# Hybrid mLSTM and attention layer: the four t1 token sums of the block products given lags of 2.7 instead of 1.5

## The chip, the cores and the metric

The kernel runs on one core of a Trainium2 chip. The metric is the device time of one execution in microseconds (us). The kernel before has three timed runs and one profiled run.

## What is computed

One step of a decoder layer, for a prompt of 1024 tokens and for 8 sample sequences of 4 tokens (32 rows), with a model width of 1024. The input is normalised and modulated (adaLN) to h. One wide product `h @ w_in` gives the inputs of two branches, an mLSTM with 4 heads and matrix memory, and sliding window attention with 8 heads; gates merge the two, and an output product closes the layer:

```python
h, gate = adaln_in(x, c, w_ada, b_ada, g_norm)
(mq, mk, mv, mi, mf, mo, mz, aq, ak, av, az, gm, ga) = split_in(h @ w_in)
y_m, C, n, m = mlstm_branch(mq, mk, mv, mi, mf, mo, mz, C0, n0, m0, b_i, b_f, g_mn)
...
y_a = o.astype(x.dtype) * jax.nn.silu(az)
u = jax.nn.sigmoid(gm) * (y_m @ w_mo) + jax.nn.sigmoid(ga) * (y_a @ w_ao)
x = x + gate * (u @ w_o)
```

Within a head the mLSTM goes through the prompt in chunks of 128 tokens. For each chunk there is a masked score product S of queries and keys, an output n from S and from the memory C, and an update U of C. The sample rows take their memory from `state_C` and `state_n` and give it back.

## The kernel before, in words

Products with large weights run in float32r at full rate with each operand split into a high and a low part (names with `h` and `l`), as three products: high by high, low by high, high by low. ACT makes a high part by a cast, and DVE the low part by a subtraction. A product of 512 columns is one PE instruction of 128 x 128 weights.

The kernel has four stages: the normalisation and the first products; direct jobs (queries and head inputs, `head_jobs`); the block products (`block_products`, from line 1493), which run from about 285 to 820 us on the profile's clock and include everything told here; and the output product.

**Block products.** The columns of `w_in` that are left are taken in pairs of 128 column blocks. The 2 x 2 form by Strassen and Winograd over halves of the contraction (kh) and of the tokens (th) needs 7 products instead of 8. They are numbered 1 to 7, and `flat` lists them in PE's order; a product is called (pair, number), as (0,5). Each has 12 matmuls: three for each of four k. Their right operands are blocks of h (b11, b21, b22) and four sums of token blocks, t1 to t4. Results stand in PSUM tiles bx, bw, by and bz; `samples` (line 1356) makes the sample rows of a pair as 16 small matmuls into `smp`, ACT copies that to `smps`, and a further small matmul makes `smpo` from it. `evac` empties a finished product: for head inputs DVE adds two parts into `mkv`, for gates ACT makes a tanh into `gt`; `gts` is the same for the sample rows. The left operands, weights (`wr_...`), come by DMA, are summed by DVE (`first_sums`, line 1370) and split into `wh_...` and `wl_...` with a number for the product.

**The token sums.** `sum_blocks` (line 1302) forms t3, t2 and t4 first, then t1. t1 is formed in place over block (0,1) of h, so it waits until the direct jobs, which read that block, are done (`products_done`, set at line 1815). Then for each of four k: ACT casts the high part, DVE subtracts it for the low part (`block_split`, line 1294), and for the first two k the loads of a later pair of `hb` tiles are issued. Behind each of the four stands a lag.

**The side work.** Between the k of a product, `side.tick` (class `Side`, lines 112 to 170) lets other work into PE's order: the heads of the mLSTM, at most two at once, the attention, the sample heads, the output weights (`out_weights`, line 1743) and `sum_blocks` itself. Each is a Python generator; what it yields is a lag and the PSUM banks of its next step. The clock of this scheduler, `now`, is a model: each matmul that is written adds its own modelled time (512 columns: 512 / 2400 us). A step is taken when its lag has passed, its banks are free by the model and 1.5 us have passed since the last one with banks. A loop holds the main products where they need a result:

```python
def until(self, done):
    while not done():
        self.now += 0.1
        self.tick()
...
if n == 0 and i in (6, 5):
    side.until(lambda: {6: "t2", 5: "t1"}[i] in formed)
```

The second part is in `hook` (line 1786), which every product calls first. So ahead of (0,5) the clock goes on in steps of 0.1 until t1 is formed, and side steps that come due meanwhile are written into PE's order there.

PE runs in the order in which the program is written (`in_order`). DVE and ACT, in this stage, are ordered by the tile scheduler from the program's order and its own estimates. All loads and stores go through SP's queue in order, and each also waits for the landing of the eighth before it. A store is held back by 8 us of the model's clock, or until its data is read.

**A head's chunk** has, on PE, tk and tv (transposes of keys and values, copied to `hk` and `hv` by ACT), S, U and n, and later ty (transposes of the output). DVE updates C from U, prepares the mask tile `et` and the weighted query `qw`, which come by DMA (`et<-nmd`, `qw<-wid`, and `hq`, `hk`, `hv`), and scales the output with a reciprocal square root in small steps (f3r_w, f3r_y). ACT takes the exponential of et. tk, tv, ty, smp, smpo and sU share one pool of two PSUM banks (pool b), so each waits until the one before the last has been copied out. A sample head has, on PE, sn (reads the memory Cs) and three sU (its update), and DVE adds them, `Cs<-Cs,sU`.

`out_weights` loads pairs of tiles `wor` and scales them by the gate on DVE (`wor<-wor,gb`).

Of the kernel before, what the change touches and what calls it, by code (L numbers as in the profile page):

```python
# [172 lines left out]
def body(tc, a):  # L173
    nc = tc.nc
    with ExitStack() as ctx:
# [810 lines left out]
        def head_jobs(h):  # L986
            q, k, v = mD[h]

            def keep(dst, smp, scale, eng):
                def ev(p, acc, c0, n):  # L990
                    t = ht([128, 384], f"mk{h}")[:, :n]
                    if eng == "v":
                        V.tensor_copy(t, acc[:, :n])
                    else:
                        S.activation(t, acc[:, :n], AF.Copy, scale=scale)
                    m = n if p < 2 else 256
                    store(dst[:, c0:c0 + m], t[:, :m])
                    if p == 2:
                        G.tensor_copy(smp[:, h], t[:, 256:288])
                return ev  # L1000

            for n, dst, smp, scale in (("mq", q, qs, float(128 ** -0.5)), ("mk", k, ks, 1.0), ("mv", v, vs, 1.0)):
                if (n, h) not in order:
                    return
                i = order.index((n, h)) - order.index(None)
                if i == -4:
                    side.add("x", sum_blocks())
                if i == -1:
                    side.finish("g")
                    sc_bank[:] = po, "o+"  # L1010
                    next(work)
                job((n, h), keep(dst, smp, scale, "s"), (lambda: next(work)) if i == -1 else None)
                head_part(h, 2)
# [273 lines left out]
        def block_load(names, k):  # L1287
            ts = []
            for kh, th in names:
                ts.append(ht([128, 512], f"hb{kh}{th}_{k}"))  # L1290
                dma(ts[-1], hD[:, 4 * kh + k, HALF[th]])
            return ts

        def block_split(n, k, t):
            hi, lo = blocks[n][k]
            S.copy(hi, t)
            V.tensor_tensor(lo, t, hi.bitcast(F32), op=ALU.subtract)

        def block_tiles(n, k):
            blocks[n].append(tuple(ht([128, 512], f"{n}{x}{k}", F32R) for x in "hl"))  # L1300

        def sum_blocks():
            names = "t3", "t2", "t4"
            for n in names:
                blocks[n] = []
            load = lambda k: block_load(((0, 0), (0, 1), (1, 0), (1, 1)), k)
            nxt = load(0)
            yield 7.0, ""
            for k in range(4):
                b11, b12, b21, b22 = nxt  # L1310
                for n in names:
                    block_tiles(n, k)
                V.tensor_tensor(b22, b22, b12, op=ALU.subtract)
                yield 2.5, ""
                V.tensor_tensor(b11, b11, b22, op=ALU.add)
                V.tensor_tensor(b21, b21, b11, op=ALU.subtract)
                yield 5.0, ""
                if k < 3:
                    nxt = load(k + 1)
                for n, t in zip(names, (b22, b11, b21)):  # L1320
                    block_split(n, k, t)
                    yield 2.5, ""
            formed.append("t2")
            load = lambda k: block_load(((0, 0), (0, 1)), k)
            ts = [load(0), load(1)]
            yield 3.0, ""
            for b11, b12 in ts:
                V.tensor_tensor(b12, b12, b11, op=ALU.subtract)
            while not products_done:
                yield 0.5, ""  # L1330
            for k in range(4):
                b11, b12 = ts[k]
                if k > 1:
                    V.tensor_tensor(b12, b12, b11, op=ALU.subtract)
                block_split("t1", k, b12)
                if k < 2:
                    ts.append(load(k + 2))
                yield 1.5, ""
            formed.append("t1")

        OPERANDS = {1: "b11", 2: "b21", 3: "b22", 4: "t4", 5: "t1", 6: "t2", 7: "t3"}
# [1 line left out]
        class Pair:  # L1343
# [6 lines left out]
            def load(self):  # L1350
                for c, n in enumerate(self.names):
                    for kh in range(2):
                        t = self.raw[c, kh] = raw_tile(f"wr_{n[0]}{n[1]}_{kh}")
                        dma(t, a["w1"][JOBS[n]][:, 4 * kh:4 * kh + 4])
# [819 lines left out]
```

## Time and profile before

| what | us |
|---|---|
| timed runs | 847.02, 848.38, 848.36 |
| median of the timed runs | 848.36 |
| the profiled run's own time | 845.97 |
| span of the profiled run | 844.1 |
| DVE busy in the span | 574.6 (68%) |
| ACT busy in the span | 399.9 (47%) |

The span goes from the first to the last instruction. The granted clock of TensorE has a mean of 0.997. Rows of a timeline give the start, the busy time, the engine and line, the operation with output and inputs, the number of instructions in the group, and in brackets how long the engine was idle ahead of it and what ended that. All operations of DVE and ACT have line 219 and the matmuls lines 258 and 263, those of the helpers that record them, so a group is known by its tiles. float32r shows as f32 in PE's rows.

### The profile page before, as it was taken

How to read it: one execution, taken by the hardware profiler on the slowest of the kernel's cores; microseconds unless marked ns; L12 is line 12 of the kernel's file. 1: busy time of each engine (PE TensorE's matmuls, PEld its weight loads, DVE VectorE, ACT ScalarE, POOL GpSimd, SP SyncE). 2: the span in 40 equal slices, each digit the busy share in tenths (PEclk: the TensorE clock that was granted, in tenths of full speed). 3: DMA queues.
4: the chain of work that ended last, by engine and by line, in shares of the span. 5: the costliest groups of instructions: out<-in, count | busy, mean ns of one | idle time of the engine just before them, and what ended most of it. 6: DMA issues, size and time to landing. Idle time of an engine off the chain costs nothing.

```text
span 844.1 us, 15344 instructions
## 1 busy us (share of the span) xinstructions
PE 826.2 (98%) x5231; PEld 692.9 (82%) x5231; DVE 574.6 (68%) x1554; ACT 399.9 (47%) x989; POOL 43.9 (5%) x77
## 2 busy tenths in 40 slices
PE   6999999999999999999999999999999999999996
PEld 3779999879988878888878777777778999997776
DVE  4887884556666586655776776788876767844676
ACT  4663346555764454554444534444444333234343
POOL 0120000000000000000000000000001202240000
PEclk9999999999999999999999999999999999999998
DMA  9996548348755653456656574555444698343532
GB/s 334 381 353 196 145 149 280 111 125 259 213 158 171 191 172 119 153 162 175 199 184 224 172 241 127 177 165 138 126 145 148 209 333 292 105 129 121 200 107 106
DMA packets 120417, 158.16 MB, mean 187 GB/s; under 512 B 27520, under 2 KB 71168, under 8 KB 120308
## 3 DMA queue, kind: packets, MB, share of 16 engines
q1 hardware_dynamic: 120196, 156.93, 58.0%
q8 instruction: 41, 0.67, 0.3%
q14 instruction: 36, 0.29, 0.1%
q10 hardware_dynamic: 144, 0.26, 0.1%
HBM read 113.41 MB, written 44.75 MB: 187 GB/s over the span
## 4 chain that ended last, share of the span: by engine, by line
PE 86%; DVE 6%; DMA 4%; issue 2%; ACT 1%; SPq 1%; DVEq 0%; ACTq 0%
PE bx L258 9%; PE by L258 8%; PE bw L258 8%; PE g_aq L258 6%; PE g_w_mo L258 6%; PE g_w_ao L258 5%; PE g_mk L258 4%; PE g_mq L258 4%; PE bz L258 4%; PE g_mv L258 3%; PE foW L258 3%; PE foX L258 3%; PE foY L258 2%; PE sc L258 2%; PE oT L258 2%; PE foZ L258 2%
## 5 line engine op out<-in xcount | busy, mean ns | idle before, releaser
L258 PE MATMUL g_w_ao<-ya,wh_w_ao 128*128 128x384 f32 (+1 forms) x192 | 45.6, 322 | 0.1
L258 PE MATMUL g_w_mo<-ym_l,wh_w_mo 128*128 128x384 f32 (+1 forms) x192 | 45.7, 323 | 0.0
L219 ACT ACTIVATE p<-p,nmx 128x256 f32<-128x256 f32 (+1 forms) x64 | 31.0, 486 | 27.0 <-DVE nmx L219 22.8
L258 PEld LDWEIGHTS g_w_ao<-ya,wh_w_ao 128*128 128x128 f32 x192 | 33.5, 188 | 0.6 <-DVE ya L219 0.4
L258 PEld LDWEIGHTS g_w_mo<-ym_l,wh_w_mo 128*128 128x128 f32 x192 | 33.5, 188 | 0.0
L258 PE MATMUL g_aq<-h_h,wh_aq 128*128 128x384 f32 (+1 forms) x96 | 32.4, 337 | 0.0
L258 PE MATMUL g_aq<-h_l,wh_aq 128*128 128x384 f32 (+1 forms) x96 | 31.0, 323 | 0.0
L258 PE MATMUL g_w_mo<-ym_l,wl_w_mo 128*128 128x384 f32 (+1 forms) x96 | 31.0, 323 | 0.0
L258 PE MATMUL g_aq<-h_h,wl_aq 128*128 128x384 f32 (+1 forms) x96 | 31.0, 323 | 0.0
L258 PE MATMUL g_w_ao<-ya,wl_w_ao 128*128 128x384 f32 (+1 forms) x96 | 30.8, 321 | 0.0
L219 DVE CUSTOM_DVE_ANT_0 p<-sc,cst,sink 128x256 f32<-128x256 f32 (+1 forms) x64 | 26.1, 464 | 3.9 <-PE sc L258 3.9
L258 PE MATMUL g_mk<-h_h,wh_mk 128*128 128x384 f32 (+1 forms) x72 | 24.8, 344 | 0.0
L258 PE MATMUL g_mq<-h_h,wh_mq 128*128 128x384 f32 (+1 forms) x72 | 24.4, 339 | 0.0
L219 ACT ACTIVATE gt<-gt 128x512 f32<-128x512 f32 (+1 forms) x17 | 10.4, 613 | 29.0 <-DVE gt L219 27.8
L258 PE MATMUL g_mk<-h_l,wh_mk 128*128 128x384 f32 (+1 forms) x72 | 23.3, 323 | 0.0
L258 PE MATMUL g_mq<-h_l,wh_mq 128*128 128x384 f32 (+1 forms) x72 | 23.3, 323 | 0.0
L258 PE MATMUL g_mk<-h_h,wl_mk 128*128 128x384 f32 (+1 forms) x72 | 23.2, 323 | 0.0
L258 PE MATMUL g_mq<-h_h,wl_mq 128*128 128x384 f32 (+1 forms) x72 | 23.2, 323 | 0.0
L219 DVE SCALAR_TENSOR_TENSOR u_h<-tgw_ao,g_w_ao 128x384 f32<-128x384 f32 (+1 forms) x24 | 12.3, 519 | 11.4 <-PE g_w_ao L258 11.0
L258 PEld LDWEIGHTS g_aq<-h_h,wh_aq 128*128 128x128 f32 x96 | 18.0, 188 | 1.4 <-issue 1.2
L219 DVE SCALAR_TENSOR_TENSOR tgw_mo<-tgw_mo,g_w_mo 128x384 f32<-128x384 f32 (+1 forms) x24 | 12.4, 518 | 9.6 <-PE g_w_mo L258 9.4
L219 ACT ACTIVATE sq<-rows_l 128x512 f32<-128x512 f32 (+2 forms) x18 | 10.6, 587 | 17.8 <-issue 12.0
(1718 smaller groups left out, 2695.8 us busy)
## 6 DMA issues: line engine op xcount, KB each, us to landing
hb<-hD SPq DMA_DIRECT2D x24, 256.0 KB
x<-xT SPq DMA_DIRECT2D x16, 256.0 KB
early_h<-w_ada SPq DMA_DIRECT2D x8, 512.0 KB
adar_ga<-w_ada SPq DMA_DIRECT2D x16, 256.0 KB
wr_ga<-w SPq DMA_DIRECT2D x16, 256.0 KB
wr_gm<-w SPq DMA_DIRECT2D x16, 256.0 KB
taD<-gt SPq DMA_DIRECT2D x16, 256.0 KB
tmD<-gt SPq DMA_DIRECT2D x16, 256.0 KB
```

What stands on the lines that cost most here:

```text
L219: ins = f(*args, **kw)
L258: in_order(nc.tensor.matmul(out, lhsT, rhs, start=start, stop=stop, skip_group_check=more))
```

## The change

One line of `sum_blocks`: the lag behind each of the four steps that form t1 is 2.7 instead of 1.5.

```diff
                 block_split("t1", k, b12)
                 if k < 2:
                     ts.append(load(k + 2))
-                yield 1.5, ""
+                yield 2.7, ""
             formed.append("t1")
```

The same instructions are written with the same shapes. Their order changes from (0,5) to the end of the sample heads; ahead of that and in the output product it is the same. Three places follow.

The first is DVE at the start of the block products, around the emptying of by (`mkv<-p,by`), which the product (0,4) needs. `et` and `qw` with `cst` and `hq` are the preparation of the next chunk. Before:

```order
L219 TENSOR_TENSOR f3r_w<-f3r_y 128x3
L219 TENSOR_TENSOR f3r_w<-f3r_w,f3v 128x3
L219 SCALAR_TENSOR_TENSOR f3r_y<-f3r_w,f3r_y 128x3
L219 TENSOR_SCALAR et<-et,f3den,f3r_y 128x128 x3
L219 TENSOR_TENSOR ws_4131<-wr_gm_0_4030,wr_gm_1_4032 128x512
L219 TENSOR_TENSOR wl_phead_in_6__3971<-wr_mk_0_3679,wh_phead_in_6__3970 128x512
L219 TENSOR_TENSOR mkv<-p_3915,by 128x512
L219 SCALAR_TENSOR_TENSOR C<-C,dec,U_1_3920 128x129 x3
```

And now:

```order
L219 SCALAR_TENSOR_TENSOR f3r_y<-f3r_w,f3r_y 128x3
L219 TENSOR_TENSOR et<-et,cst 128x256
L219 TENSOR_TENSOR f3r_w<-f3r_y 128x3
L219 SCALAR_TENSOR_TENSOR C<-C,dec,U_1_3898 128x129
L219 TENSOR_TENSOR f3r_w<-f3r_w,f3v 128x3
L219 TENSOR_TENSOR qw<-qw,hq_2_3911 128x256
L219 SCALAR_TENSOR_TENSOR f3r_y<-f3r_w,f3r_y 128x3
L219 SCALAR_TENSOR_TENSOR C<-C,dec,U_1_3898 128x129
L219 TENSOR_SCALAR et<-et,f3den,f3r_y 128x128 x3
L219 TENSOR_TENSOR ws_4152<-wr_gm_0_4033,wr_gm_1_4035 128x512
L219 TENSOR_TENSOR wl_phead_in_6__3988<-wr_mk_0_3679,wh_phead_in_6__3987 128x512
L219 TENSOR_TENSOR mkv<-p_3943,by 128x512
```

The updates of C, which stood behind mkv, stand ahead of it (the first of the three just ahead of these rows), and one et and one qw as well, which stood some rows further on.

The second is ACT in the last chunk of head 3, in the products of a gate pair; gts is the copy of smpo and frees its bank. Before:

```order
L219 CAST wh_pgate_3__5307<-wr_ga_1_4902 128x512
L219 COPY by<-bw 128x512
L219 ACTIVATE gts<-smpo 128x64
L219 ACTIVATE et<-et,an 128x128 x2
L219 ACTIVATE yt<-ty_0_5268,vec 128x384
L219 CAST wh_pgate_4__5331<-wr_gm_1_4906 128x512
```

And now:

```order
L219 ACTIVATE et<-et,an 128x128 x2
L219 CAST wh_pgate_3__5307<-wr_ga_1_4908 128x512
L219 COPY by<-bw 128x512
L219 ACTIVATE gts<-smpo 128x64
L219 ACTIVATE yt<-ty_0_5258,vec 128x384
L219 CAST wh_pgate_4__5332<-wr_gm_1_4912 128x512
```

The two exponentials of et, which stood behind gts, stand ahead of wh_3, by and gts.

The third is PE at the first sample head, in the products of pair 6's gate. Before:

```order
L258 MATMUL smp<-wr_gm_0_5961,c_102 32x128
L258 MATMUL smp<-wr_gm_1_5963,c_102 32x128
L258 MATMUL sU_0_6056<-vm_5859,skn 128x388
L258 MATMUL sU_1_6059<-vm_5864,skn 128x388
L258 MATMUL by<-t3h_2714,wh_pgate_7__5965 128x512
L258 MATMUL by<-t3l_2715,wh_pgate_7__5965 128x512
L258 MATMUL by<-t3h_2714,wl_pgate_7__5966 128x512
```

And now:

```order
L258 MATMUL bx<-h_h_576,wl_pgate_2__5935 128x512
L258 MATMUL sU_0_6028<-vm_5848,skn 128x388
L258 MATMUL sU_1_6031<-vm_5853,skn 128x388
L258 MATMUL bx<-h_h_576,wh_pgate_2__5934 128x512
L258 MATMUL bx<-h_l_577,wh_pgate_2__5934 128x512
L258 MATMUL bx<-h_h_576,wl_pgate_2__5935 128x512
L258 MATMUL smp<-wr_ga_0_5981,c_102 32x128
```

The first two sU stood behind the 16 matmuls of smp (the first two rows are the last of these); now they stand three matmuls ahead of smp (the last row is its first matmul). On DVE the addition `Cs<-Cs,sU` follows the fourth `wor<-wor,gb` directly; before, a `wl` and a weight sum stood between them. On SP, the loads of a head's next chunk and the weight loads have changed places: in head 3 the loads hq, hk, hv, et and qw now follow directly on `wr_ga` of pair 5's first half, ahead of a store of tmD and of its second half, which stood ahead of them before; and the last pair of hb loads for t1 now stands behind the second half of pair 0's gate weight `wr_ga`, where it stood ahead of it.

## The prediction

> **What bounds the kernel now.** I read the page first, then the waits of PE, then the timelines of the engines around each place that the change moves. The page has PE busy for 826.2 of 844.1 us at a granted clock that stays at nine tenths or more in all slices but the last:
>
> ```profile
> PE 826.2 (98%) x5231; PEld 692.9 (82%) x5231; DVE 574.6 (68%) x1554; ACT 399.9 (47%) x989; POOL 43.9 (5%) x77
> ...
> PEclk9999999999999999999999999999999999999998
> ```
>
> So PE sets the end: a matmul that waits costs its whole wait, and a wait on another engine costs only where PE's row stands behind it. From 280 to 830 us, which holds everything that the change moves, PE waits three times (the columns are total, times, longest):
>
> ```profile
> PE smp L258 <- ACT hv L219: 1.9, 1, 1.9
> PE bx L258 <- ACT gt L219: 0.5, 1, 0.5
> PE sU L258 <- DVE Cs L219: 0.2, 1, 0.2
> ```
>
> That is 2.6 us. No more than this, and the price of switching between kinds of matmul, can be gained. What can be lost is not bounded so: the three rows say that all other waits just fit now.
>
> **What the change does.** It adds no instruction's work and removes none. The four lags only move the side clock: while the loop in `hook` waits for t1 at product (0,5), the clock is pushed ahead by up to 4.8 us more (4 x 1.2), so every side block behind it becomes due earlier. On PE, the blocks of the heads stand three to ten matmuls ahead of where they stood, until the sample heads end. The operands of these blocks come from DVE, ACT and SP, whose order moves too. Six places have a price.
>
> *1. The first product with t4, by(0,4).* PE ends bw(0,3) and then waits a little for DVE's `mkv`, which empties `by`:
>
> ```profile
> 307.37 0.69 DVE L219 TENSOR_TENSOR mkv<-p,by 128x512 f32<-128x512 f32 x1
> 307.97 1.12 DVE L219 SCALAR_TENSOR_TENSOR C<-C,dec,U 128x129 f32<-128x129 f32 x3
> ```
>
> ```profile
> 307.59 0.39 PE L258 MATMUL bw<-h_h,wl_phead_in__3879 128*128 128x512 f32 x1
> 308.11 0.50 PE L258 MATMUL by<-t4h,wh_phead_in__3898 128*128 128x512 f32 x1
> ```
>
> bw's last matmul holds PE for 0.23 us (the spacing shown under 4), to 307.82; by starts at 308.11, so 0.29 is lost. Now three updates of C (1.03 from 307.97 to the next operation), one `et` and one `qw` (0.43 each, by the row of that shape under 5) stand ahead of `mkv` on DVE: 1.9 in all. Part of it falls into the chain of small f3r steps, each of which waits for the one before it, so I take half, 0.9: mkv ends at 308.95. PE meanwhile has ty_0, 0.33, ahead of by instead of inside it, and comes to by at 308.15. The loss is 0.85 instead of 0.29: **+0.6**. Bounds: all hidden, -0.3; nothing hidden, +1.6.
>
> *2. tv of head 2, chunk 0*, now directly behind smp and tk, needs the bank that ACT frees by copying smps; tk's three matmuls cover 0.33 of that copy and its start. **+0.2**, between 0 and 0.4.
>
> *3. Gate pair 0.* n, tk, tv and S of head 2, chunk 1 now stand three matmuls ahead of smp instead of behind it, and smp takes the bank that `hv<-tv` frees. This is the mechanism of the 1.9 us wait above. How long hv takes from tk shows one chunk later in the kernel before (ACT, then PE):
>
> ```profile
> 321.44 0.35 ACT L219 COPY hv<-tv 128x256 f32<-128x256 f32 x1
> ...
> 325.56 0.48 ACT L219 COPY hv<-tv 128x384 f32<-128x384 f32 x1 [1.92 <-PE tv L263]
> ```
>
> ```profile
> 319.82 0.38 PE L263 MATMUL tk<-cst,hk 128*128 128x128 f32 x2
> ```
>
> From tk to the end of hv are 321.79 - 319.82 = 1.97, and 0.13 more for the copy of three parts. PE's own tk, tv, S and three matmuls come to about 2.0. **+0.2**, from 0 up to 0.7 if ACT is late.
>
> *4. Fewer switches.* The first 512 column matmul behind a block of small ones has its next 0.32 behind it, all others 0.23:
>
> ```profile
> 418.14 0.48 PE L258 MATMUL bw<-t2h,wh_pgate__5147 128*128 128x512 f32 x1
> 418.46 0.39 PE L258 MATMUL bw<-t2l,wh_pgate__5147 128*128 128x512 f32 x1
> 418.69 0.40 PE L258 MATMUL bw<-t2h,wl_pgate__5148 128*128 128x512 f32 x1
> ```
>
> The changed order has five such blocks fewer (they now follow another block directly). 5 x 0.09: **-0.45**. That is certain, since the order is fixed.
>
> *5. Head 3, last chunk, around 416 to 427 us.* SP's queue, DVE, ACT and PE before:
>
> ```profile
> 415.22 0.33 SPq L246 DMA_DIRECT2D wr_ga<-w  x1
> ...
> 418.43 0.42 SPq L246 DMA_DIRECT2D et<-nmd  x1
> ```
>
> ```profile
> 424.21 0.43 DVE L219 TENSOR_TENSOR et<-et,cst 128x256 f32<-128x256 f32 x1 [5.95 <-DMA et<-nmd]
> ```
>
> ```profile
> 418.93 0.62 ACT L219 CAST wh_pgate__5307<-wr_ga 128x512 fp32r<-128x512 f32 x1
> 419.46 0.58 ACT L219 COPY by<-bw 128x512 f32<-128x512 f32 x1
> 419.97 0.21 ACT L219 ACTIVATE gts<-smpo 128x64 f32<-128x64 f32 x1
> 424.67 0.70 ACT L219 ACTIVATE et<-et,an 128x128 f32<-128x128 f32 x2 [4.49 <-DVE et L219]
> ```
>
> ```profile
> 422.34 0.30 PE L258 MATMUL smp<-wr_ga,c 128*32 128x128 f32 x2
> ```
>
> The load of et, issued at 418.43, reaches DVE at 424.21: 5.78 us. ACT took wh_3, by and gts while it was under way. In the changed order ACT has the two `et` activations ahead of these three, so ACT stands still until et has landed; gts frees the bank of smp, so PE stands still with it. The load itself is issued earlier: on SP it now follows that wr_ga at 415.22 by four issues of some 0.45, so at about 417.0. From landing to gts pass 0.46 (DVE), 0.60 (two et), 0.53 (wh), 0.51 (by), 0.21 (gts) and the release: 2.35. With 5.78 from issue to landing, smp would start at 417.0 + 5.8 + 2.35 = 425.1 instead of 422.34, 2.8 later. The shortest time of such a load is in these two rows (SP, DVE), 3.83:
>
> ```profile
> 310.61 0.41 SPq L246 DMA_DIRECT2D et<-nmd  x1
> ```
>
> ```profile
> 314.44 0.56 DVE L219 TENSOR_TENSOR et<-et,cst 128x384 f32<-128x384 f32 x1 [1.75 <-DMA et<-nmd]
> ```
>
> With that, 423.2: 0.85 later. One 256 KB transfer fewer is ahead of it than at 418.43, so I take 4.4, nearer to the short row: 423.75, 1.4 later. The wait of 0.5 of bx on gt, a few matmuls on, goes, since that gt then comes in time. **+0.9**, between +0.35 and +2.3; nothing below unless the load lands sooner than any such row shows.
>
> *6. Sample head 0, around 485 to 496 us.* SP, DVE and PE before:
>
> ```profile
> 484.78 1.90 SPq L246 DMA_DIRECT2D wor<-w_out  x4
> ```
>
> ```profile
> 490.83 1.29 DVE L219 TENSOR_TENSOR wor<-wor,gb 128x512 f32<-128x512 f32 x2 [3.09 <-DMA wor<-w_out]
> 492.04 0.69 DVE L219 TENSOR_TENSOR wl_pgate__6063<-wr_ga,wh_pgate__6062 128x512 fp32r<-128x512 f32 x1
> 492.64 1.29 DVE L219 TENSOR_TENSOR wor<-wor,gb 128x512 f32<-128x512 f32 x2
> ...
> 495.05 0.55 DVE L219 TENSOR_TENSOR Cs<-Cs,sU 128x387 f32<-128x387 f32 x1
> ```
>
> ```profile
> 491.42 0.30 PE L258 MATMUL smp<-wr_ga,c 128*32 128x128 f32 x2
> ...
> 492.43 0.95 PE L258 MATMUL sU<-vm,skn 96*128 96x388 f32 x2
> ```
>
> Before, smp ran at 491.42 and the two sU behind it. Now the two sU stand three matmuls ahead of smp, and smp takes the bank of the first, which DVE frees with `Cs<-Cs,sU`. That addition is queued on DVE behind four `wor` operations, and DVE waits 3.09 us for their transfer. SP issues these loads behind the same weight loads as before, so they land at the same distance from PE's products. The fourth wor ends at 493.85 (492.64 + 1.29, less their overlap); Cs ends at 494.4. PE comes to smp at 491.42 + 0.8 for the two sU = 492.2. It waits 2.25; sU's own 0.2 goes: **+2.1**. Had the loads landed in 3.8 us, as the shortest above, the wait would be gone (-0.2); landing half a us later makes it +2.6, a full one +3.1.
>
> Other moved blocks have a margin in the order that the rows give (0.3 us at the nearest), and I count them at nothing; where one of these covers fails, it costs some tenths.
>
> **The sum**: 0.6 + 0.2 + 0.2 - 0.45 + 0.9 + 2.1 = +3.55 against the profiled execution, whose own time is 845.97 us (span 844.1 and 1.9 around it), so 849.5. That execution lies 2.4 below the median of the three timed runs, 848.36, which is what is forecast: 848.36 + 3.55 = **851.9 us**. About 0.2%, 1.7 us, is what a measurement of this kernel can tell from no change.
>
> **Rivals.** *No change.* Both transfers land early enough, so 5 and 6 turn from +3.0 into the two small waits that go, -0.5 and -0.2. The sum is then 0.55 - 0.7 = -0.15: 848.2 us. Against it stands that wor took 6.05 us from its first issue to DVE, and was waited for; for it, that terms 5 and 6 each rest on one transfer whose time I know from one execution. The Trainium skill (page "DMA: Bandwidth & Descriptors", section "Anatomy of one DMA — SWDGE (gpsimd) path") gives 2.0 us plus the bytes at 436 GB/s for a DMA of the GpSimd path: an estimate of 2.3 us for et's 128 KB and 2.6 for a wor, with which no wait would appear at either place. The trace disagrees with that in both (5.78, 6.05): with several transfers in flight a load waits for others. I go by the rows: 0.24 for this case, with the one in which only the wait for wor goes (+1.25).
>
> *Faster.* The 1.9 us wait of smp for hv goes as well, because h's casts on ACT come in another rhythm. With the two small waits and the switches that is 1.9 + 0.7 + 0.45 = 3.05: 845.3 us. It decides on where hv stands on ACT, and that speaks against it: the same rows stand ahead of hv as before (two h_h casts, mkv, the copy of n and its three squares), and the loads that the casts wait for are issued at the same place. 0.10.
>
> *Much slower.* t1 itself comes late. The last pair of loads for t1 now stands behind a weight load on SP that waits for DVE; the chain of waits shows how long the first of them took, and when the last parts were done:
>
> ```profile
> 286.01 7.02 DMA hb<-hD
> ...
> 299.20 1.20 DVE h_l L219 x2
> ```
>
> PE needs the last part at about 304.4 and I work out its end at 302.3. If the last pair takes the 7.02 of the first from an issue near 294, it lands at 301 and the part is ready at 303 to 304; with a full queue on DVE it overtakes PE. Each us beyond costs one, say 2: 848.36 + 3.55 + 2 = 853.9. 0.06. The Trainium skill (page "TensorE: Matmul & The Clock Gate", section "What's actually happening") says that an idle window of about 3.4 us halves PE's clock; by that rule two of my waits run together would cost more than their length. The 1.9 us wait left the clock row above at nine, which agrees as far as it goes; no run here shows a longer one.
>
> **How the numbers follow.** The forecast itself 0.60; no change 0.24; faster 0.10; much slower 0.06. The forecast's own range goes from 5 at its lower end and 6 a us below my value (0.55 + 0.35 + 1.1 = 2.0: 850.4) to both at their upper ends (0.55 + 2.3 + 3.1 = 5.95: 854.3). For 8 in 10 I take in "no change" with 0.3 below it, and leave out the faster case and the upper half of the much slower one: **847.9 to 854.4 us**. Slower by over 0.2% is the forecast and the much slower case less what of the former falls short: 0.64. Within 0.2%: 0.26. Faster: 0.10.
>
> **What would show it right or wrong.** In the waits of PE in the profile after: a wait of smp on gts at 423 us of some 1.4; a wait of smp on Cs near 493 of some 2.2; by on mkv near 309 grown by some half a us; smp on hv still 1.9. No such waits at the two smp rows would break the forecast, as would a 1.9 that is gone. A wait of bz on h_l would be the much slower case.

## The result, and the profile after

| | before | after |
|---|---|---|
| median of five timed runs, us | 848.17 (847.02 to 848.38) | 853.26 (851.58 to 855.38) |
| the profiled run's own time, us | 845.97 | 851.58 |
| its span, us | 844.1 | 849.8 |

The change makes the kernel slower: the ratio is 1.0063, with a 95% interval of 1.0048 to 1.0079. The forecast was 851.9 us.

The page after, its row of PE and its row of the granted clock:

```profile
PE 826.1 (97%) x5231; PEld 693.0 (82%) x5231; DVE 574.8 (68%) x1554; ACT 400.3 (47%) x989; POOL 43.7 (5%) x77
...
PEclk9999999999999999999999999999999999999998
```

PE works as long as before and its clock is the same, so the 5.7 us that the span has grown are waits. The waits of PE after, from 280 to 840 us (total, times, longest):

```profile
PE bw L258 <- ACT bw L219: 1.9, 2, 1.4
PE smp L258 <- ACT hv L219: 1.8, 1, 1.8
PE smp L258 <- ACT gts L219: 1.5, 1, 1.5
PE smpo L258 <- ACT hv L219: 1.2, 1, 1.2
PE bx L258 <- ACT gt L219: 1.2, 1, 1.2
PE smp L258 <- DVE Cs L219: 1.0, 1, 1.0
```

They add up to 8.6 us against 2.6 before, 6.0 more; less the 0.45 of the switches that are saved, 5.55 of the 5.7 are accounted for. The timeline of PE puts them in their places (start, busy, operation, and in brackets the wait):

```profile
296.91 0.30 PE L258 MATMUL smp<-wr_mk,c 128*32 128x128 f32 x2 [1.77 <-ACT hv L219]
...
320.26 0.43 PE L258 MATMUL smpo<-cst,smps 128*128 128x64 f32 x2 [1.23 <-ACT hv L219]
...
425.36 0.30 PE L258 MATMUL smp<-wr_ga,c 128*32 128x128 f32 x2 [1.50 <-ACT gts L219]
...
443.67 0.50 PE L258 MATMUL bw<-t2h,wh_pgate__5433 128*128 128x512 f32 x1 [0.49 <-ACT bw L219]
...
467.29 0.51 PE L258 MATMUL bw<-t2h,wh_pgate__5672 128*128 128x512 f32 x1 [1.37 <-ACT bw L219]
...
497.42 0.30 PE L258 MATMUL smp<-wr_ga,c 128*32 128x128 f32 x2 [0.99 <-DVE Cs L219]
...
525.02 0.50 PE L258 MATMUL bx<-h_h,wh_pquery_gate__6238 128*128 128x512 f32 x1 [1.20 <-ACT gt L219]
```

The first wait was there before. The two at 425 and 497 were forecast; the four at 320, 444, 467 and 525 were not, and they are 4.3 us. All of them have one form: what PE waits for is short (a copy on ACT, at 497 the addition `Cs<-Cs,sU` on DVE), and it, or the DVE operation that feeds it, stands behind something that has nothing to do with it.

**At 320 us** hv, which frees a bank of pool b, stands behind the exponentials of et. The load of et on SP, its first use on DVE, and ACT:

```profile
311.22 0.44 SPq L246 DMA_DIRECT2D et<-nmd  x1
```

```profile
316.98 0.56 DVE L219 TENSOR_TENSOR et<-et,cst 128x384 f32<-128x384 f32 x1 [4.50 <-DMA et<-nmd]
```

```profile
317.58 0.99 ACT L219 ACTIVATE et<-et,an 128x128 f32<-128x128 f32 x3 [2.64 <-DVE et L219]
318.47 0.46 ACT L219 COPY et<-n 128x387 f32<-128x387 f32 x1
...
319.86 0.35 ACT L219 COPY hv<-tv 128x256 f32<-128x256 f32 x1
```

The load took 5.76 us to its use (316.98 - 311.22), where the same load took 3.83 before. ACT stood still for 2.64 of them.

**At 425 us** it is the same, as forecast:

```profile
418.30 0.38 SPq L246 DMA_DIRECT2D et<-nmd  x1
```

```profile
423.02 0.42 DVE L219 TENSOR_TENSOR et<-et,cst 128x256 f32<-128x256 f32 x1 [3.89 <-DMA et<-nmd]
```

```profile
423.48 0.69 ACT L219 ACTIVATE et<-et,an 128x128 f32<-128x128 f32 x2 [4.46 <-DVE et L219]
...
425.10 0.21 ACT L219 ACTIVATE gts<-smpo 128x64 f32<-128x64 f32 x1
```

From issue to use are 4.72 us; the prediction took 4.4.

**At 444 and 467 us** ACT's copy `bw<-bx` stands behind the tanh `gt<-gt`, which waits for DVE's `gt<-p,bw`; on DVE, operations on wor now stand ahead of that. At 444 these are two `wor<-wor,gb`, and DVE comes to them only after 3.10 us of waiting for a weight load (`wr_gm<-w`); gt follows at 441.78. DVE and ACT at 467:

```profile
460.74 0.69 DVE L219 TENSOR_TENSOR wor<-wor,wor 128x512 f32<-128x512 f32 x1 [2.17 <-DMA woDb<-wor]
461.35 0.15 DVE L219 SCALAR_TENSOR_TENSOR f2den<-et 128x2 f32<-128x2 f32 x1
461.47 0.69 DVE L219 TENSOR_TENSOR wor<-wor,wor 128x512 f32<-128x512 f32 x1
...
465.41 0.68 DVE L219 TENSOR_TENSOR gt<-p,bw 128x512 f32<-128x512 f32 x1
```

```profile
466.12 0.63 ACT L219 ACTIVATE gt<-gt 128x512 f32<-128x512 f32 x1 [5.30 <-DVE gt L219]
466.66 0.58 ACT L219 COPY bw<-bx 128x512 f32<-128x512 f32 x1
```

Before, that `gt<-p,bw` stood ahead of the first `wor<-wor,wor`:

```profile
459.67 0.68 DVE L219 TENSOR_TENSOR gt<-p,bw 128x512 f32<-128x512 f32 x1
...
461.01 0.68 DVE L219 TENSOR_TENSOR wor<-wor,wor 128x512 f32<-128x512 f32 x1
```

Now DVE waits 2.17 us for a store that the first of these needs, and then does the four of them between the small steps of the f2 chain: gt comes at 465.41.

**At 497 us** the forecast mechanism is there, with a smaller price. SP and DVE:

```profile
488.67 1.91 SPq L246 DMA_DIRECT2D wor<-w_out  x4
```

```profile
493.08 0.69 DVE L219 TENSOR_TENSOR wor<-wor,gb 128x512 f32<-128x512 f32 x1 [1.50 <-DMA wor<-w_out]
...
495.61 1.29 DVE L219 TENSOR_TENSOR wor<-wor,gb 128x512 f32<-128x512 f32 x2
496.82 1.02 DVE L219 TENSOR_TENSOR Cs<-Cs,sU 128x387 f32<-128x387 f32 x2
```

The first wor reached DVE 4.41 us after its issue (493.08 - 488.67), against 6.05 before (490.83 - 484.78), so the four wor and Cs come that much sooner against PE, less 0.63 us for which the second wor waits for its own load.

**At 525 us** `gt<-bx` on ACT stands behind three casts `vm<-vf` of the next sample head, each of which waits for DVE and not for a transfer; before, it ran at 514.81 and the first of them at 519.50, behind it:

```profile
523.56 0.41 ACT L219 CAST vm<-vf 32x258 fp32r<-32x258 f32 x1 [0.87 <-DVE vf L219]
...
524.39 0.58 ACT L219 ACTIVATE gt<-bx 128x512 f32<-128x512 f32 x1
```

### The profile page after: what moved, and what is told of

It reads as the page before. It is cut to its first block, busy times and chain, and to the rows that moved or that the text cites. A ratio compares the mean times of both kernels' runs of the same rounds, so it can differ in the third digit from the quotient of the medians.

```text
span 849.8 us, 15333 instructions
## 1 busy us (share of the span) xinstructions
PE 826.1 (97%) x5231; PEld 693.0 (82%) x5231; DVE 574.8 (68%) x1554; ACT 400.3 (47%) x989; POOL 43.7 (5%) x77
## 4 chain that ended last, share of the span: by engine, by line
PE 85%; DVE 6%; DMA 5%; issue 2%; ACT 1%; SPq 1%; DVEq 0%; ACTq 0%
PE by L258 9%; PE bx L258 8%; PE bw L258 8%; PE g_aq L258 6%; PE g_w_mo L258 5%; PE g_w_ao L258 5%; PE g_mk L258 4%; PE g_mq L258 4%; PE bz L258 4%; PE g_mv L258 3%; PE foW L258 3%; PE foX L258 3%; PE foY L258 2%; PE sc L258 2%; PE oT L258 2%
## 5 line engine op out<-in xcount | busy, mean ns | idle before, releaser
L219 ACT ACTIVATE et<-et,an 128x128 f32<-128x128 f32 x32 | 10.9, 393 | 24.3 <-DVE et L219 24.3
```

The source lines that it names most:

```text
L219: ins = f(*args, **kw)
```

## The experiments

**The theories.** A: the longer lag only pushes the scheduler's clock, the push moves blocks ahead on PE and re-sorts ACT and DVE, and PE then waits where a copy stands behind an instruction that waits for a transfer. Its first part, A1, is ACT behind et (320 and 425 us); its second, A2, is DVE behind wor (444, 467 and 497 us). The wait at 525 us is in neither part. The rival B: t1 itself, its parts and the loads behind it come later, and that costs the time. "Before" in a ratio is the kernel before on the same chip.

**1. The push without the lag** (`e1_push_only`). The kernel before; at (0,5) the clock is pushed ahead by 3.1 us, which is what the longer lags bring by the model. In the trace PE's order is that of the changed kernel, and the orders of ACT and SP are nearly so.

```diff
                 side.until(lambda: {6: "t2", 5: "t1"}[i] in formed)
+                if i == 5:
+                    end = side.now + 3.1
+                    side.until(lambda: side.now >= end)
```

> The lags stay 1.5, so t1 is formed as in the kernel before, and the side clock is pushed ahead by 3.1 us at (0,5), as far as the changed kernel's loop pushes it (263.58 to 266.72 on the model's clock). Theory A, that the push alone costs: about 853 us like the changed kernel (851.6 to 855.4), with its seven waits of PE (8.6 us in the block products). Rival B, that the wider spacing of t1's own steps costs: 848 us, with the three waits of before (2.6 us).

Measured: 855.09 us, ratio 1.0087 (1.0072 to 1.0103); PE waits at six of the changed kernel's places (hv 2.2, smpo 0.7, gts 2.5, bw 1.7 at 470 us, Cs 1.1, gt 1.2), and behind hv and gts its clock is at half for a while (see the last section).

**2. The lag without the push** (`e2_no_push`). The lag is 2.7, but the last steps of t1 are taken directly at (0,5), so the clock stays.

```diff
-                yield 1.5, ""
+                yield 2.7, ""
...
-                side.until(lambda: {6: "t2", 5: "t1"}[i] in formed)
+                if i == 6:
+                    side.until(lambda: "t2" in formed)
+                while i == 5 and "t1" not in formed:
+                    side.step(side.streams["x"]["live"][0])
```

> The lags are 2.7 and t1's last steps are written at (0,5) as in the changed kernel, but the model's clock does not go on there. Theory A: 848 us as before, three waits of PE, 2.6 us in all. Rival B: 853 us as the changed kernel.

Measured: 849.75 us, ratio 1.0012 (0.9997 to 1.0027). In the trace PE's order is that of the kernel before, while t1 is as slow as in the changed kernel: from its first cast `h_h<-hb` to the end of its last `h_l` pass 8.2 us in both, and 6.5 before. So the push alone brings the whole loss, and the lag without it none that can be told: B falls, and of A the part holds that the push is what costs. The 2.0 of bx on gt is the old one of 0.5, near 430 us; of the new kinds there is only a bw of 0.6:

```profile
PE smp L258 <- ACT hv L219: 2.1, 1, 2.1
PE bx L258 <- ACT gt L219: 2.0, 1, 2.0
PE bw L258 <- ACT bw L219: 0.6, 1, 0.6
```

**3 and 4. Other lengths of the push** (`e3_lag_2_2`, `e4_lag_3_5`): the lag of the changed kernel at 2.2 and at 3.5, by the model pushes of 1.1 and 6.3 us.

```diff
-                yield 2.7, ""
+                yield 2.2, ""
```

> Lag 2.2: the loop pushes the model's clock by about 1.1 us instead of 3.1. If the loss grows with the push (blocks ahead by a given distance lose their margin one by one), some 850 us, with the waits of the changed kernel smaller or fewer. If each order is its own draw, anything from 847 to 854, with waits at other places.

> Lag 3.5: the loop pushes the clock by about 6.3 us. PE's order differs little from the changed kernel's (200 lines against 2,430 from before). If the loss grows with the push, 855 or more; if it follows the order, near the changed kernel's 853 with nearly the same waits.

Measured: 853.72 us, 1.0049 (1.0029 to 1.0068), and 852.86 us, 1.0036 (1.0019 to 1.0053). Each has its own waits: at 2.2 one of 3.6 of ty on yt and one of 1.8 of smpo on hv, none of gts or Cs; at 3.5 one of 3.3 on gts. The loss does not grow with the push. That the order which comes out decides instead is read from the different waits, and not tested by itself.

**5. A1 taken away** (`e5_et_first`). The changed kernel with the loads of et and qw ahead of those of hq, hk and hv, so that they land earlier.

```diff
                 w_[p] = [ht([128, 512], f"h{n}{h}_{p}") for n in "qkv"]
-                for t, d in zip(w_[p], mD[h]):
-                    dma(t[:, :w], d[:, c0:c0 + w])
                 e_, qw = ht([128, 512], "et"), ht([128, 3, 128], "qw")
...
                     dma(t, st[d][j0:j0 + m].unsqueeze(0).to_broadcast((128, m, 128)))
+                for t, d in zip(w_[p], mD[h]):
+                    dma(t[:, :w], d[:, c0:c0 + w])
```

> The changed kernel, with each head chunk's et and qw loaded ahead of hq, hk and hv instead of behind them, some 1.4 us earlier on SP. Theory A1, that smp waits for gts at 425 us, and smpo for hv at 320, because ACT stands still for the load of et: both waits (1.5 and 1.2) fall below 0.5, and the time by 2 us to about 851. Rival: the load lands when the whole group of loads has landed, whatever its place in it: both waits stay and the time is 853.

Measured: 850.85 us, 1.0032 (1.0017 to 1.0046), half of the loss. The waits at 320 and 425 are gone, and the old one on hv is down to 0.2. Those at 444 and 467 are gone too, although wor still stands ahead of gt there, so the half that was won is not A1's alone. Three others appear:

```profile
PE smp L258 <- DVE Cs L219: 1.5, 1, 1.5
PE ty L263 <- ACT yt L219: 1.4, 1, 1.4
PE bx L258 <- ACT gt L219: 1.2, 1, 1.2
PE ty L263 <- DVE et L219: 0.9, 1, 0.9
PE bw L258 <- DVE t2l L219: 0.7, 1, 0.7
PE smp L258 <- ACT hv L219: 0.2, 1, 0.2
```

**6. A2 taken away by moving it** (`e6_wor_gpsimd`). The 24 operations on wor in `out_weights` on GpSimd instead of DVE (V becomes G in five lines, the first of them shown).

```diff
-                    V.tensor_tensor(t, t, gb[f], op=ALU.mult)
+                    G.tensor_tensor(t, t, gb[f], op=ALU.mult)
```

> The changed kernel, with the output weights' multiplications and sums done by GpSimd instead of DVE; the order of PE and ACT is the same. Theory A2, that bw waits for ACT's copy at 444 and 467 us (0.5 and 1.4) and smp for Cs at 497 (1.0) because DVE's queue has wor operations, which wait for DMAs, ahead of gt and Cs: the three waits go, 2.9 us, to about 850.5. Rival: the small reciprocal root steps of the heads, which stand there too, hold gt back: the first two waits stay, and only the third goes, 852.

Measured: 864.57 us, 1.0197 (1.0181 to 1.0213). Nothing of what was expected held: PE waits three times for bw, 8.7 us in all. GpSimd, and DVE beside it, around 467 us:

```profile
466.63 5.37 POOL L219 TENSOR_TENSOR wor<-wor,wor 128x512 f32<-128x512 f32 x4 [4.77 <-DMA woDb<-wor]
```

```profile
466.70 1.25 DVE L219 TENSOR_TENSOR f2r_w<-f2r_w,f2v 128x2 f32<-128x2 f32 x1
467.99 0.16 DVE L219 SCALAR_TENSOR_TENSOR f2r_y<-f2r_w,f2r_y 128x2 f32<-128x2 f32 x1
468.18 1.14 DVE L219 TENSOR_TENSOR f2r_w<-f2r_y 128x2 f32<-128x2 f32 x1
...
472.77 0.68 DVE L219 TENSOR_TENSOR gt<-p,bw 128x512 f32<-128x512 f32 x1
```

While GpSimd works, every other small step of DVE takes 1.1 to 1.25 us instead of 0.16, so gt, behind the chain, comes at 472.77. The chain also starts 3.0 us later than in the changed kernel, at 464.35, as DVE waits 4.27 us for a weight load (`wr_gm<-w`) ahead of it. The run does not separate A2 from its rival, as the cure costs more than the ill.

**7. A2 taken away by leaving the work out** (`e8_no_wor_ops`). The changed kernel without the 24 operations on wor; the output product then uses weights that are neither scaled nor summed, so its time says only what these operations cost on DVE.

```diff
                 for (k, f), t in raws.items():
-                    V.tensor_tensor(t, t, gb[f], op=ALU.mult)
...
-                    V.tensor_tensor(b22, b22, b12, op=ALU.subtract)
```

> The changed kernel without the output weights' 24 multiplications and sums (its output product uses unscaled weights); loads and stores stay, PE's and ACT's order is the same. Theory A2 (DVE's wor operations hold gt and Cs back): bw's waits for ACT's copy near 444 and 467 us (0.5 and 1.4) and smp's for Cs near 497 (1.0) go, the waits of smp for gts, smpo for hv and bx for gt stay; about 850.5 us. Rival (the chain of small reciprocal root steps ahead of gt holds it): the wait near 467 stays above 1, the time above 852.

Measured: 849.68 us, 1.0001 (0.9982 to 1.0019). The waits at 444, 467 and 497 are gone, with hv (2.2), smpo (1.1), gts (0.8) and gt (1.2) left, and three of 0.4 to 0.7 besides. The copies of bw end at 443.02 and 464.39; PE in the changed kernel was ready for them at 443.18 and 465.92, so they would be in time there too, and A2 holds. The time falls by more than these three waits (2.85 us), so it is not theirs alone: gts, for one, went from 1.5 to 0.8.

**8. The loads of et first, in the kernel before** (`e7_et_first_before`). The edit of 5 without the change.

> The kernel before (lags 1.5), with et and qw loaded ahead of hq, hk and hv. PE's order is that of before. In the changed kernel this took the first wait of smp for hv from 1.8 to 0.2. If the same holds here, that wait of 1.9 and bx's 0.5 go: 846 us, the best of all. Rival: the scheduler's new order of ACT and DVE costs as much elsewhere: 848.

Measured: 851.31 us, 1.0020 (1.0004 to 1.0036). This is a miss. hv falls to 1.1, but PE waits 3.5 us for ty's bank at 424.53, and its clock is halved behind that. PE's row and, below, stretches of the run (length, PE busy and its matmuls, granted clock, DMA share, GB/s):

```profile
424.53 0.69 PE L263 MATMUL ty<-cst,et 128*128 128x128 f32 x2 [3.54 <-ACT yt L219]
```

```profile
424.50:428.00 3.50, 3.47 (x13) 0.50 0.77 262
428.00:432.00 4.00, 4.00 (x41) 0.71 0.75 231
```

**9 and 10. et in its turn** (`e9_et_in_turn` from the changed kernel, `e9b_et_in_turn_before` from the one before). On ACT an edge of order holds the exponentials of et behind the instruction that the program writes ahead of them, so the scheduler cannot put them ahead of the copies.

```diff
+                    elif self.name == "S":
+                        i = getattr(ins, "ins", ins)
+                        if behind and "written" in last:
+                            no_sync(i, [last["written"]])
+                        last["written"] = i
...
+                behind.append(1)
                 for i in range(len(GROUPS[p])):
                     S.activation(et[:, i], et[:, i], AF.Exp, bias=an[:, j0 + i:j0 + i + 1])
+                behind.clear()
```

> The changed kernel, with ACT's exponentials of et held behind the ACT instruction written ahead of them, so that on ACT they stand behind gts in head 3 and not ahead of it; PE's order is the same, and the loads of et too. Theory A1 (ACT stands still for the load of et with the emptying of a bank behind it): smp's wait for gts near 425 us (1.5) goes, and the first wait of smp for hv (1.8) gets shorter, since hv then stands ahead of the later h_h casts; smpo's wait for hv near 320 (1.2) stays, because there the exponentials still stand ahead of hv; the waits for wor (444, 467, 497) stay. About 850.5 us. Rival: PE waits for something that lands as late whatever ACT does first; no change, 853.

> The same hold in the kernel before; PE's order is that of before. If A1 holds, bx's wait for gt (0.5) and most of smp's for hv (1.9) go: 846 to 847 us, the best of all. If the scheduler's new places for the exponentials meet other waits, as with the loads in another order, 848 to 850.

Measured: 853.4 us, 1.0051 (1.0034 to 1.0067), and 848.94 us, 0.9988 (0.9973 to 1.0002). In the first the wait at 425 is gone: gts runs at 423.46, ahead of the exponentials at 426.66, and A1 holds there. Against the expectation the wait at 320 is gone as well; the exponentials are done there by 316.3, so this agrees with A1. That the wait at 467 is gone says nothing about A2: the four wor still stand ahead of gt, but PE, which has lost time further ahead, comes to bw at 469.08, behind the copy. ty now waits 1.65 us for et at 308, and bw 1.83 at 445, and the time stays. In the second bx no longer waits for gt, but hv waits 3.2. Neither gains what was hoped for.

**11. The clock put back** (`e10_back_3`). The kernel before, with the clock put back by 3.0 us at (0,5), the opposite of the change.

```diff
+                if i == 5:
+                    side.now -= 3.0
```

> The kernel before (lags 1.5) with the model's clock set back by 3 us at (0,5), so that the side blocks come due later instead of earlier. If only blocks that stand earlier lose their margin, waits get fewer and the time is 848 or less. If any other order costs, since the margins of before were found for its own order, 850 or more, with new waits at other places.

Measured: 850.17 us, 1.0009 (0.9997 to 1.0021): another order with other waits (hv 2.1, bw 1.1, ty 1.0, a bx on zt 0.9), and no gain.

**12. The squares behind the copies** (`e12_squares_behind`). The kernel before; the three squares `mjk` of a chunk, which stand ahead of hv on ACT, are written behind the next chunk's hv and hk (the visits of `load`, `prep` and the stages take a new step `squares`).

```diff
                 S.copy(ns[:, :m], num[:, :m])
+                w_[p] = ns
+
+            def squares(p):
+                m, ns = len(GROUPS[p]), w_[p]
                 ssq = sm([128, 3], "mssq", 2)
```

> The kernel before, with the squares of a chunk's output (mjk, three on ACT, 0.3 each) written behind the next chunk's hv and hk instead of ahead of them; PE's order is that of before. The wait of smp for hv near 297 us, which both kernels have (1.9 and 1.8), shrinks by the 0.9 of the three squares. If nothing behind the squares becomes late: 0.9 below before. Rival: the squares' own followers (the small root steps, the scaled et, ty) now come 1.5 us later and PE waits there; no gain.

Measured: 848.68 us, 1.0007 (0.9988 to 1.0025). hv falls from 1.9 to 1.4, and by waits 1.0 for mkv and gt 1.7 instead: moved, not saved. No version is measurably faster than the kernel before.

**The account over all runs.** For the profiled execution of each kernel, against that of before (2.6 us of waits, span 844.1): the waits of PE from 280 to 840 us, the time that the granted clock falls short of full (its missing share times the length, over stretches of 5 us), their sum, and what the span has grown. All in us:

| kernel | waits more | clock lost | sum | span longer |
|---|---|---|---|---|
| after | 6.0 | 0 | 6.0 | 5.7 |
| 1 push only | 6.8 | 3.4 | 10.2 | 9.2 |
| 2 no push | 2.1 | 3.4 | 5.5 | 5.3 |
| 3 lag 2.2 | 5.3 | 1.7 | 7.0 | 8.5 |
| 4 lag 3.5 | 5.9 | 3.4 | 9.3 | 7.3 |
| 5 et first | 3.3 | 0 | 3.3 | 3.1 |
| 6 wor on GpSimd | 13.7 | 6.9 | 20.6 | 19.7 |
| 7 no wor operations | 4.4 | 0 | 4.4 | 4.5 |
| 8 et first, before | 3.0 | 3.4 | 6.4 | 5.4 |
| 9 et in turn | 5.1 | 3.4 | 8.5 | 7.6 |
| 10 et in turn, before | 2.5 | 1.7 | 4.2 | 5.3 |
| 11 clock put back | 3.5 | 1.8 | 5.3 | 4.4 |
| 12 squares behind | 1.7 | 0 | 1.7 | 1.8 |

Waits and clock together give the span to 1.1 us, but for 3 and 4 (1.5 short, 2.0 over). One profiled execution is not the median. The one of before in this table, 845.97 us, is faster than each of the 35 runs of that kernel on the chip of 3, 4, 7 and 8 (846.54 to 852.98), which is why 7 stands at +4.5 here and at a ratio of 1.0001 above. What waits an ordinary execution of before has is not on record. For the change itself the two are alike, as its profiled execution, 851.58, is the fastest of its five as well. The clock is part of that spread, as the last section shows.

## Why the prediction was right, and where it was not

The direction and the kind of cause were right, and the time lies in the range, but the sum of 3.55 was too small against the 5.7 of the profile and the 5.1 between the medians. Step by step:

- *1, by(0,4), +0.6*: nothing. bw's last matmul starts at 307.78 and by at 308.25, 0.47 later, against 0.52 before. All that moved ahead of mkv fell into the gaps of the f3r chain, not half of it.
- *2, +0.2*: it came, though it is too short for the list of waits: tv starts 0.50 us behind tk (324.99 - 324.49), as it waits for ACT's copy of smps, and 0.33 behind it before (325.04 - 324.71).
- *3, +0.2*: nothing. Up to 407 us the products of the gate pairs stand 1.36 to 1.45 later than before at the points where PE's order is the same again, and that is in place at 328 us, ahead of them.
- *4, -0.45*: it stands in the account above, which closes with it to 0.15, about what step 2 cost.
- *5, +0.9*: right in place, mechanism and size. The wait is 1.50 against the 1.4 forecast, and the 0.5 of bx on gt went. The times themselves are later than in the text, by 1.3 us for et's issue and 1.5 for PE, which nearly cancel.
- *6, +2.1*: the mechanism is right, the size is not. The wait is 0.99 instead of 2.25, since the loads of wor landed after 4.41 us and not after 6.05 at the "same distance". The text had the end at 3.8 us, where nothing would be left; the truth lay between, and the value taken was the row at one end.
- *"Other moved blocks have a margin ... and I count them at nothing"*: this is the step that failed. Four waits arose there, 1.23 + 0.49 + 1.37 + 1.20 = 4.3 us. The margins were read from PE's rows and the order of the copies, as if what stands ahead of a copy on ACT or DVE kept its time. But of these four, the first (1.23) has the mechanism of step 5 at another et, two (0.49, 1.37) have that of step 6 at other wor operations, and the last (1.20) has ACT behind vm. A mechanism found at one place should have been looked for at each place where its instruction stands.

The errors have opposite signs: 1 + 3 + 6 were 0.8 + 1.3 too high (6 came to 0.99 - 0.2 = 0.8), and the step that failed 4.3 too low. That the forecast came within 1.4 us of the median is in part luck: of the 3.0 us forecast for 5 and 6 together 1.8 came, and the places counted at nothing brought more than both.

Of the rivals, *faster* needed the wait on hv to go, and it is still 1.77. *Much slower* needed t1 to be late: no bz waits for h_l, and experiment 2 shows that a later t1 costs nothing that can be told. *No change* needed early loads at both places; one of the two came 1.6 us earlier than I took, and it was not enough. The changed kernel's profile shows no fall of the clock, so nothing of its 5.7 is owed to that; in the experiments it is a large part of the time.

What stays open: the causes at 425 (9) and at 444, 467 and 497 (7) are shown, and 320 agrees with its own (5, 9). For the wait at 525 no experiment takes the cause away; it is 1.20 to 1.22 in each kernel with the changed kernel's order of PE, exact or nearly so (1, 4, 5, 6, 7, 9), and missing in all others. No way was found to foretell which order of ACT and DVE is good. Where one wait was taken away (5, 8, 9, 10, 12), others arose, and which of them a given edit brings was seen only afterwards. One reason is that waits do not add up freely: a wait makes PE late and so covers the next place, as in 1 at 444 and in 9 at 467, where gt still stands behind wor and PE no longer waits. That an order without any of them exists wasn't tried.

## What to carry to other kernels

Where a scheduler's clock decides the order, a lag is not a local number: pushing it re-sorts every queue behind it, and the tuned margins go. To cost such a change, list every instruction on ACT and DVE that waits for a transfer or for another engine, and for each see what PE needs behind it in the new order, not only at the places where PE's own order looks tight. And count a wait of PE above some 1.6 us at more than its length.

## What the runs showed of the hardware

**A wait of 1.65 to 2.2 us can halve TensorE's clock, and one of 2.5 always did.** In run 2 the old wait on hv is 2.1 us, and the clock behind it falls, where before (1.9) and after (1.8) it did not. Run 2, then before:

```profile
295.00:300.00 5.00, 2.92 (x39) 0.91 0.79 276
300.00:305.00 5.00, 5.00 (x19) 0.75 0.41 128
```

```profile
295.00:300.00 5.00, 3.10 (x42) 1.00 0.53 188
300.00:305.00 5.00, 5.00 (x26) 1.00 0.23 80
```

0.09 x 5 + 0.25 x 5 = 1.7 us are lost. Over the profiles of all fourteen kernels, from 280 to 840 us, none of the waits of 1.5 us or less is followed by such a dip, 7 of the 15 from 1.6 to 2.3 are, and all 8 of 2.5 and more; the loss is 1.7 each time, and 3.4 behind the 4.72 of run 6 and the 3.54 of run 8. The Trainium skill (page "TensorE: Matmul & The Clock Gate", section "What's actually happening") has the clock halved after an idle window of about 3.4 us that runs freely. The loss of 1.7, half of 3.4, agrees with its length, and the places of the dips agree with a free run: in run 1 they start at 299.0, 428.7 and 848.5 us, 38 and 123 times 3.413 us apart. That shorter waits are enough differs from the page; there the measurement decides.

The profiles fit a rule in which it counts how much of a wait falls into one such window. In run 1 the wait of 2.21 us on hv lies whole in the window that ends at 299.0, and the clock falls; in run 6 a wait of the same length is cut by the edge of a window at 296.5 into 0.89 and 1.32, and it does not. With the edges laid out from the dips of each profile, 15 of the 16 windows with 1.65 us or more of waits are followed by the half clock (the other one has 1.83, in run 7), and from full clock none with 1.5 or less. By that rule the same wait would cost one execution and not the next, and the executions of one kernel do differ: in 27 runs of the kernel before on the chip of 9, 10 and 11 the mean granted clock goes from 0.993 to 0.999, and the span from 844.7 us (at 0.999) to 849.5 (at 0.994 and 0.995).

**GpSimd holds up DVE's small operations.** In run 6 an operation of 128x512 took 1.34 us on GpSimd (5.37 / 4) where DVE takes 0.69, and while it ran, every other one of DVE's steps of 128x2 took 1.1 to 1.25 us instead of 0.16: nearly as long as GpSimd's operation. The Trainium skill (page "SBUF — State Buffer", section "Who interferes with whom") says that a DVE instruction with two SBUF inputs contends with a GpSimd instruction that reads SBUF; the rows agree, with a whole operation of GpSimd as the price.

**The same load takes 3.8 to 5.8 us.** et reached DVE 3.83 and 5.78 us after its issue before, 5.76 and 4.72 after, and wor 6.05 and 4.41. In this kernel a margin under some 2 us at a load is no margin.
